# Three changes of order in a one-core encoder layer: a bank's read among the last quarter's scalings, three couples of differences at later blocks, and one more piece of filler in two turns of a scan

## The chip, the cores and the metric

The kernel runs on one core of a Trainium2 chip. The time is that of one execution on the device, in microseconds (us). Three runs of the kernel before gave 2434.46, 2435.89 and 2437.45; the median is 2435.89. The profile is of a further execution.

## The reference

One step of a one-layer hybrid encoder on 1024 new tokens of a prompt and 64 tokens of a running stream, which the kernel treats as T = 1088 columns; D = 1024. Cut to what matters:

```python
proj = rmsnorm(x) @ w_in                      # z | xBC | dt | q | k | v | g_ssm | g_att
xs, b, c = split(silu(causal_conv(xBC)))      # conv of width 4
for chunk in chunks_of_64(t):                 # state-space scan, 4 groups of 8 heads
    y     = (c b^T * decay) @ (dt x) + (c @ state) * exp(acum)
    state = state * exp(acum_end) + b^T @ (to_end * dt x)
y   = rmsnorm_per_group((y + d * xs) * silu(z))
o   = rmsnorm(differential_attention(q, k, v))
mix = sigmoid(g_ssm) * (y @ w_branch_ssm) + sigmoid(g_att) * (o @ w_branch_attn)
x   = x + mix @ w_out
ha, hb = split(rmsnorm(x) @ w_up)             # 2 x 2816 wide
x   = x + (silu(causal_conv(ha)) * hb) @ w_down
```

## The kernel before

Matrices lie with features on the 128 partitions and tokens along the free axis. Every large product is done in three passes of TensorE (PE): each operand is split into a high and a low part (a cast on ScalarE, ACT, L155 or L419, and a subtraction on VectorE, DVE, L156 or L420), and high x high, high x low and low x high are summed in one bank. A product in the text below is one matmul of 272 columns (a quarter of T). The in-projections of q, k and z, the up-projection and the down-projection also use a seven-product scheme for 2 x 2 blocks (`PARTS`), which needs differences of the four blocks as operands.

A scheduler sets the order of each engine's instructions from the program and from priorities; `issue_after` (the helper `after`) pins an instruction behind another. The queues of DMA issues are on SyncE (SP); each works in order.

**Scan** (about 1087 to 1498 us). Twelve spans: four groups `g`, each over three stretches of tokens of 384, 384 and 320 (`WIDE`). A span has three steps of a chunk of 128 tokens (the last one 64), and one more turn at its end, 48 turns in all. For a chunk, `front` transposes x (`tr`, L1280, and `xx`, L1289), forms the small product `cb` (L1282, L1283) and the decays `bc` (L1290 to L1293); `back` makes `yi` (L1301), `ye` (L1307) and the state's update `stp` (L1313, L1320), and puts y together (L1308, L1309). At a span's end `gated` adds d x (L1327), multiplies by silu(z) on GpSimd (POOL, L1328), squares (L1329) and sums (L1330, L1331); `normed` sums over partitions on PE (`gst`, L1335) and takes the root (L1338, L254 to L258); `scaled` scales (L1345) and stores y to `y_sc` (L1348 for groups 2 and 3; L1354 to L1357, with a split, for groups 0 and 1). Tile `y` has two buffers.

After each turn, `fill` takes work from a generator `filler` and issues it as PE work beside the scan: first the rest of the gates, then branch 1 (attention's output by its weights) and branch 2 (the first two groups of `y_sc` by theirs). A piece is 24 products (L170 to L172), and a turn takes 1.4 x 363 / 272 = 1.87 pieces on average. What is left runs after the scan, and then branch 3 (groups 2 and 3 of `y_sc`, loaded at L218 as b, split at L419 and L420), whose operations end in tanh gates on ACT (L226).

**Norm and up-projection** (about 1712 to 2190 us). `norm(q)` for each quarter of the tokens is a generator: the root, a pause, then eight scalings (L1527). `differences(s)` makes the block differences (L1537 to L1546) and their splits. `pair(f)` works through the 14 products groups (p, s) of one pair of blocks (L1612); its banks are copied or read by DVE, the read of p = 1 at L1639.

**Down-projection** (about 2182 to 2427 us). Three groups of 8, 8 and 6 feature blocks; four output blocks for each, twelve values of `i`, about 22 us each in the first two groups. Right operands for a group are loaded by `right_part` (L1721) from `h_sc` (plain) or `t_sc` (differences), in units called n, m and ph; ph shares its buffers (tag "fb") with the tile `ht`. `differences_of` makes the differences for a couple of blocks: load ht (L1689), two differences (L1693, L1694), two more (L1697, L1698), store to `t_sc` (L1700). The last three couples, which only the third group of the down-projection reads, are made during i = 0, 1 and 2. Banks are read at L1791, L1796, L1798, L1800, L1805 and L1808.

Of the kernel before, what the change touches and what calls it, by code (L numbers as in the profile page):

```python
# [12 lines left out]
ALU = mybir.AluOpType  # L13
# [6 lines left out]
KT = D // P  # L20
# [70 lines left out]
def hybrid_layer(ctx: ExitStack, tc: tile.TileContext, xT, xt, prm, cst, rope, wvd, win, wbs, wba, wout, wup, wdn,  # L91
# [31 lines left out]
    def col(o):  # L123
        return par[:, o : o + 1]
# [1123 lines left out]
    with (tc.tile_pool(name="sin", bufs=1) as sin, tc.tile_pool(name="sp", bufs=1) as sp,  # L1248
# [169 lines left out]
        def branch_tiles():  # L1418
            nonlocal bs
            cv_pool.release()  # L1420
            bs = tc.alloc_tile_pool(name="bs", bufs=1, side="right")
            yield from branch(True, side, o_sc, wba, D, (), store(m_sc))
            yield from branch(True, side, y_sc[: 2 * D], wbs[0], None, (), store(n_sc))

        bs, late = None, chain(filler, branch_tiles())
        for i in scan():
            if i == BRANCH_AT and late is not None:
                filler, late = late, None
            fill(SCAN_STEPS)
        load(out=conv, in_=conv_o)  # L1430
    dq.release()
    psf = ctx.enter_context(tc.tile_pool(name="psf", bufs=1, space=PSUM))
# [84 lines left out]
    def norm(q):  # L1517
        ps = psf.tile([P, 512], F32, name="st2", tag="st2")[:, :QW]
        for i, s in enumerate(sums[q]):
            PE.matmul(ps, ones, s, start=i == 0, stop=i == 1)  # L1520
        t = [row("fu", "n2") for _ in range(2)]
        rs = t[1][:, :QW]
        rstd_of(rows, rs, ps, QW, "n2", 1.0 / D, t=t)
        yield
        for k in range(KT):
            x = x1[q][k // 4][:, k % 4]
            V.scalar_tensor_tensor(x, x, col(O_FFN + k), rs, ALU.mult, ALU.mult)  # L1527

    def part(name, s, src):
        hi, lo = B[name, s] = [unit(*at) for at in home[name, s]]  # L1530
# [54 lines left out]
        left[0].update(coming)  # L1585
        run(firsts)
    next(fourth)
    run(fourth)
    run(differences(1))


    made.clear()
# [75 lines left out]

    early = [(p, s) for p in (0, 2) for s in range(2)]
    rest = [[(p, s) for p in (1, 3, 4, 5, 6)] for s in range(2)]  # L1670
    coming = up_parts(1)
    pairs = [begun(0), begun(1)]
    for at in early + rest[0]:
        pairs[0].send(at)
    for _ in range(2):
        more_left(1)
# [166 lines left out]
    for i in range(4 * len(DOWN)):  # L1843
# [8 lines left out]
        for at, (p, s) in enumerate(steps):  # L1852
            u.send((p, s))
            lefts_at(FT + i, at, blocks, token_major)
            if last:
                next(ahead_of)
            landed()
            if i in (0, 1, 2) and at in (1, 8, 10):
                if at == 1:
                    made_now = differences_of(*couples[len(couples) - 3 + i])  # L1860
                next(made_now, None)
        run(made_now)
        del left[FT + i]
# [106 lines left out]
```

## Time and profile before

| | us |
|---|---|
| runs | 2437.45, 2435.89, 2434.46 |
| profiled execution | 2433.65 |
| its span | 2431.9 |
| PE busy | 2390.7 |
| DVE busy | 1716.9 |
| ACT busy | 1213.1 |
| POOL busy | 692.3 |

Busy means that an instruction of the engine is running; a wait is time in which an engine's next instruction stands behind another engine or a transfer. "Granted clock" is the share of full TensorE speed in a stretch; over the whole span it was 0.996.

### The profile page before, as it was taken

The numbers are of one execution on the slowest core, as the hardware profiler recorded it, in microseconds if no ns is written. First come the engines' busy times: TensorE is split into PE (matmuls) and PEld (weight loads), VectorE is DVE, ScalarE is ACT, GpSimd is POOL, SyncE is SP. The second block draws the span as 40 slices with busy tenths as digits, with TensorE's granted clock in tenths as the row PEclk, the third lists the DMA queues.
The fourth block names the chain that finished last, engine by engine and source line by source line (L and its number), as shares of the span: only waits on it lengthen the run. The fifth ranks groups of instructions, "written<-read, shape, count | busy, mean of one in ns | idle before, by whom it ended". The sixth has DMA issues, their size and how long they took to land. (4 is left out here: it accounts for less than half of the span.)

```text
span 2431.9 us, 49445 instructions
## 1 busy us (share of the span) xinstructions
PE 2390.7 (98%) x18744; PEld 2317.6 (95%) x18744; DVE 1716.9 (71%) x3090; ACT 1213.1 (50%) x2683; POOL 692.3 (28%) x757
## 2 busy tenths in 40 slices
PE   8999999999999999999999999999999999999998
PEld 8999999999999999998899998999999999999998
DVE  4678887668687786867678665756866756777765
ACT  7344454356565665657655553434444333353442
POOL 0032433201011010115343332013254554443344
PEclk9999999999999999999999999999999999999999
DMA  7863768665444444336797954664124424357975
GB/s 244 278 236 129 268 204 302 197 194 155 155 150 152 127 149 142 108 127 227 261 329 248 334 177 162 213 210 159 56 85 147 156 97 157 126 185 211 254 182 105
DMA packets 296240, 449.79 MB, mean 185 GB/s; under 512 B 36729, under 2 KB 192514, under 8 KB 296002
## 3 DMA queue, kind: packets, MB, share of 16 engines
q1 hardware_dynamic: 284962, 420.31, 52.3%
q0 software_dynamic: 11040, 26.34, 5.3%
q8 instruction: 147, 2.41, 0.4%
q14 instruction: 91, 0.75, 0.1%
HBM read 294.03 MB, written 152.50 MB: 184 GB/s over the span
## 5 line engine op out<-in xcount | busy, mean ns | idle before, releaser
L170 PE MATMUL mm<-b,w_hi 128*128 128x272 f32 x1576 | 465.8, 296 | 0.0
L172 PE MATMUL mm<-b,w_lo 128*128 128x272 f32 x1576 | 459.3, 292 | 0.0
L171 PE MATMUL mm<-b,w_hi 128*128 128x272 f32 x1576 | 458.0, 291 | 0.0
L170 PEld LDWEIGHTS mm<-b,w_hi 128*128 128x128 f32 x1576 | 296.9, 188 | 6.2 <-issue 5.1
L171 PEld LDWEIGHTS mm<-b,w_hi 128*128 128x128 f32 x1576 | 297.1, 189 | 2.9 <-issue 2.1
L172 PEld LDWEIGHTS mm<-b,w_lo 128*128 128x128 f32 x1576 | 296.5, 188 | 0.7 <-issue 0.2
L996 DVE SCALAR_TENSOR_TENSOR cc<-pre,par,cc 128x272 f32<-128x272 f32 (+1 forms) x288 | 140.0, 490 | 16.0 <-ACT cc L994 13.0
L1612 PE MATMUL mx<-n,wh 128*128 128x272 f32 x1080 | 144.9, 290 | 1.9 <-DVE u L1639 1.2
L1612 PE MATMUL mx<-m,w_hi 128*128 128x272 f32 x752 | 144.6, 289 | 0.2 <-DVE m L420 0.2
L984 POOL COPY pre<-pre 128x3 f32<-128x3 f32 x72 | 22.9, 318 | 418.5 <-DVE cc L998 198.4
L1612 PEld LDWEIGHTS mx<-n,wh 128*128 128x128 f32 x1080 | 139.7, 190 | 2.3 <-DVE u L1639 1.4
L170 PE MATMUL mx<-b,w_hi 128*128 128x272 f32 x472 | 138.8, 294 | 1.1 <-ACT w_hi L155 0.5
L172 PE MATMUL mx<-b,w_lo 128*128 128x272 f32 x472 | 137.7, 293 | 1.0 <-DVE w_lo L156 1.0
L1120 ACT ACTIVATE p_t<-sc,mx 128x512 f32<-128x512 f32 (+6 forms) x144 | 106.2, 740 | 64.4 <-DVE mx L1111 30.7
L156 DVE TENSOR_TENSOR w_lo<-w_f,w_hi 128x1024 fp32r<-128x1024 f32 (+1 forms) x82 | 102.2, 1247 | 50.6 <-ACT w_hi L155 49.6
L420 DVE TENSOR_TENSOR wh<-w_f,wh 128x512 fp32r<-128x512 f32 (+1 forms) x144 | 136.7, 950 | 0.7 <-ACT wh L419 0.7
L171 PE MATMUL mx<-b,w_hi 128*128 128x272 f32 x472 | 135.8, 288 | 0.0
L155 ACT CAST w_hi<-w_f 128x1024 fp32r<-128x1024 f32 (+1 forms) x82 | 85.9, 1048 | 70.0 <-PE mm L171 49.3
L1612 PEld LDWEIGHTS mx<-m,w_hi 128*128 128x128 f32 x752 | 118.1, 188 | 0.4 <-DVE m L420 0.4
L563 POOL TENSOR_TENSOR ws<-w_f 128x512 f32<-128x512 f32 (+1 forms) x47 | 63.1, 1342 | 176.4 <-DMA w_f<-in_wdn_dram 61.7
L1621 ACT ACTIVATE cc<-pre,par 128x544 f32<-128x544 f32 (+1 forms) x44 | 37.2, 846 | 147.9 <-DVE pre L1656 147.2
L1612 PE MATMUL mx<-m,w_lo 128*128 128x272 f32 x376 | 108.3, 289 | 0.0
(460 smaller groups left out, 7074.3 us busy)
## 6 DMA issues: line engine op xcount, KB each, us to landing
w_f<-in_win_dram SPq DMA_DIRECT2D x48, 512.0 KB, 4.3
w_f<-in_wup_dram SPq DMA_DIRECT2D x80, 256.0 KB, 2.6
bc<-a_sc SPq DMA_DIRECT2D x32, 512.0 KB, 5.6
w_f<-in_win_dram SPq DMA_DIRECT2D x60, 256.0 KB, 3.8
b<-y_sc SPq DMA_DIRECT2D x24, 544.0 KB, 8.3
h_sc<-hb SPq DMA_DIRECT2D x44, 272.0 KB, 2.1
ht<-h_sc SPq DMA_DIRECT2D x22, 544.0 KB, 4.5
t_sc<-ht SPq DMA_DIRECT2D x22, 544.0 KB, 2.9
```

The costliest lines, as they stand in the source:

```text
L155: S.copy(hi, w)
L156: V.tensor_tensor(out=lo, in0=w, in1=hi, op=ALU.subtract)
L170: PE.matmul(ps, a_hi, b_hi, start=i == 0, stop=False)
L171: PE.matmul(ps, a_hi, b_lo, start=False, stop=False)
L172: PE.matmul(ps, a_lo, b_hi, start=False, stop=i == n - 1)
L420: V.tensor_tensor(out=lo, in0=src, in1=hi, op=ALU.subtract)
L563: G.tensor_tensor(out=s1, in0=q21, in1=q22, op=ALU.add)
L984: G.tensor_copy(pre[:, 0:3], tail)
L996: V.scalar_tensor_tensor(cc[:, :m], pre[:, i : i + m], cw(i), cc[:, :m], ALU.mult, ALU.add)
L1120: act(p_t[:n, :nk], sc[c][:n, :nk], AF.Exp, bias=mx[:n, c : c + 1], accum_out=dst)
L1612: PE.matmul(ps, w[x][:, c], b[y][:, k], start=start and k == i == 0, stop=k == 3 and i == 2, skip_group_check=not start)
L1621: act(cc[:, :n], pre[h][:, :n], AF.Identity, bias=col(O_FB + f), scale=cw(0))
```

## The change

Three edits. They leave every product and every operand as it was.

1. In the scan, turns 3 and 5 take one piece of filler more.
2. In the norm of the fourth quarter there is a pause ahead of the fifth scaling, and that scaling is pinned behind the last bank's read. The program runs this second half, and the differences that follow it, only after five product groups of the first pair have been issued.
3. The last three couples' differences are made during i = 1, 2 and 5 instead of 0, 1 and 2.

```diff
-        bs, late = None, chain(filler, branch_tiles())
+        bs, late, turn = None, chain(filler, branch_tiles()), 0
         for i in scan():
             if i == BRANCH_AT and late is not None:
                 filler, late = late, None
-            fill(SCAN_STEPS)
+            turn += 1
+            fill(SCAN_STEPS + (272 / UNIT if turn in (3, 5) else 0))
...
         for k in range(KT):
+            if q == 3 and k == KT // 2:
+                yield
             x = x1[q][k // 4][:, k % 4]
-            V.scalar_tensor_tensor(x, x, col(O_FFN + k), rs, ALU.mult, ALU.mult)
+            with after("read") if q == 3 and k == KT // 2 else ExitStack():
+                V.scalar_tensor_tensor(x, x, col(O_FFN + k), rs, ALU.mult, ALU.mult)
...
     next(fourth)
-    run(fourth)
-    run(differences(1))
+    next(fourth)
...
+    pairs = [begun(0), begun(1)]
+    for at in early + rest[0][:1]:
+        pairs[0].send(at)
+    run(fourth)
+    run(differences(1))
     coming = up_parts(1)
-    pairs = [begun(0), begun(1)]
-    for at in early + rest[0]:
+    for at in rest[0][1:]:
         pairs[0].send(at)
...
-            if i in (0, 1, 2) and at in (1, 8, 10):
+            if i in (1, 2, 5) and at in (1, 8, 10):
                 if at == 1:
-                    made_now = differences_of(*couples[len(couples) - 3 + i])
+                    made_now = differences_of(*couples[len(couples) - 3 + (1, 2, 5).index(i)])
```

In the built program the lines behind the first edit are one higher than before, those behind the second four, and those behind the new block of the program from three to seven.

PE at the end of the scan, before: the back half of the scan's last chunk, with products of branches 1 and 2 (b) on both sides of it. Ninety-six products follow it ahead of the last gst (L1335), and then 120 more ahead of branch 3.

```order
9264 L172 MATMUL mm<-b_17767,w_lo 128x272
9265 L170 MATMUL mm<-b_17767,w_hi 128x272
9266 L171 MATMUL mm<-b_17768,w_hi 128x272
9267 L172 MATMUL mm<-b_17767,w_lo 128x272
9268 L1301 MATMUL yi<-bc,xx 64x64 x8
9269 L1307 MATMUL ye<-in,start 128x64 x4
9270 L1313 MATMUL stp<-xx,b_cb 128x512
9271 L170 MATMUL mm<-b_17773,w_hi 128x272
9272 L171 MATMUL mm<-b_17774,w_hi 128x272
9273 L172 MATMUL mm<-b_17773,w_lo 128x272
```

The same engine at the same place in the changed kernel. Rows 9480 and following are already products of branch 3 (b_19320 and b_19330); the last product of branch 2 is row 9473.

```order
9472 L171 MATMUL mm<-b_17594,w_hi 128x272
9473 L172 MATMUL mm<-b_17593,w_lo 128x272
9474 L1280 MATMUL tr<-con,in 128x128 x4
9475 L1282 MATMUL cb<-con,in 128x128
9476 L1283 MATMUL cb<-in 128x128
9477 L1307 MATMUL ye<-in,state 128x128 x4
9478 L1313 MATMUL stp<-xx,b_cb 128x512
9479 L1301 MATMUL yi<-bc,xx 64x128 x8
9480 L170 MATMUL mm<-b_19320,w_hi 128x272
9481 L171 MATMUL mm<-b_19321,w_hi 128x272
```

A little later in the changed kernel the last two chunks' back halves and the gst of the last span but one (384 wide) stand together; the gst of the last span (320 wide) follows at row 9526.

```order
9506 L172 MATMUL mm<-b_19320,w_lo 128x272
9507 L1313 MATMUL stp<-xx,b_cb 128x512
9508 L1307 MATMUL ye<-in,state 128x128 x4
9509 L1335 MATMUL gst<-zin,con 128x384
9510 L1313 MATMUL stp<-xx,b_cb 128x512
9511 L1301 MATMUL yi<-bc,xx 64x128 x8
9512 L1307 MATMUL ye<-in,start 128x64 x4
9513 L1301 MATMUL yi<-bc,xx 64x64 x8
9514 L170 MATMUL mm<-b_19322,w_hi 128x272
```

So the products of branches 1 and 2 now all stand ahead of the last three chunks' back halves, where before 216 of them stood behind the last one.

DVE at the fourth quarter's norm, before: the eight scalings (L1527), a weight's split (L420) among them, then the read of the bank (L1639).

```order
1968 L1527 SCALAR_TENSOR_TENSOR x_21174<-x_21174,par,n_21811 128x272 x4
1969 L1527 SCALAR_TENSOR_TENSOR x_21639<-x_21639,par,n_21811 128x272
1970 L420 TENSOR_TENSOR w_lo<-ws_21681,w_hi 128x512
1971 L1527 SCALAR_TENSOR_TENSOR x_21639<-x_21639,par,n_21811 128x272 x3
1972 L1639 TENSOR_TENSOR u_21855<-mx,u_21854 128x272
1973 L1537 TENSOR_TENSOR x_20630<-x_21174,x_20630 128x1088
```

The same in the changed kernel, where the scaling's line is L1531, the read's L1642 and the first difference's L1541:

```order
1961 L1531 SCALAR_TENSOR_TENSOR x_21174<-x_21174,par,n_21811 128x272 x4
1962 L1531 SCALAR_TENSOR_TENSOR x_21639<-x_21639,par,n_21811 128x272
1963 L420 TENSOR_TENSOR w_lo<-ws_21681,w_hi 128x512
1964 L1531 SCALAR_TENSOR_TENSOR x_21639<-x_21639,par,n_21811 128x272 x2
1965 L1642 TENSOR_TENSOR u_21826<-mm,u_21825 128x272
1966 L1531 SCALAR_TENSOR_TENSOR x_21639<-x_21639,par,n_21811 128x272
1967 L1541 TENSOR_TENSOR x_20630<-x_21174,x_20630 128x1088
```

The read now stands ahead of the last scaling.

SP's queue ahead of the third group of the down-projection, before: no load of ht is left, and loads of parts from t_sc and h_sc alternate.

```order
1263 L1721 DMA m_29193<-h_sc 128x3x272
1264 L1721 DMA m_29196<-t_sc 128x3x272
1265 L552 DMA w_f<-in_wdn_dram 128x512 x11
1266 L552 DMA w_f<-in_wdn_dram 128x384 x2
1267 L1721 DMA m_29215<-t_sc 128x3x272
1268 L552 DMA w_f<-in_wdn_dram 128x384
1269 L1721 DMA ph<-h_sc 128x3x272
1270 L1721 DMA ph<-t_sc 128x3x272
```

In the changed kernel (ht at L1696, its store at L1707, parts at L1728):

```order
1248 L1728 DMA m_29193<-h_sc 128x3x272
1249 L552 DMA w_f<-in_wdn_dram 128x512 x11
1250 L552 DMA w_f<-in_wdn_dram 128x384 x3
1251 L1696 DMA ht<-h_sc 128x1088 x2
1252 L552 DMA w_f<-in_wdn_dram 128x384
1253 L1728 DMA ph<-h_sc 128x3x272
1254 L1728 DMA n_29292<-h_sc 128x3x272
1255 L1728 DMA n_29311<-h_sc 128x3x272
1256 L1707 DMA t_sc<-ht 128x1088 x2
1257 L1728 DMA m_29375<-h_sc 128x3x272
1258 L1728 DMA ph<-t_sc 128x3x272
1259 L1728 DMA n_29272<-t_sc 128x3x272
```

The third couple's loads and stores have moved to here, and every load from t_sc for this group stands behind them.

## The prediction

> **What bounds the kernel now.** I read the page's span and busy times first, then TensorE's waits, then stretches around each wait, then the timeline there. The page:
>
> ```profile
> span 2431.9 us, 49445 instructions
> PE 2390.7 (98%) x18744; PEld 2317.6 (95%) x18744; DVE 1716.9 (71%) x3090; ACT 1213.1 (50%) x2683; POOL 692.3 (28%) x757
> ```
>
> TensorE (PE) is busy 98% of 2431.9 us, so an order can win only from 41 us without PE work and from the clock, and can lose wherever it lets PE run into work that isn't ready. The change keeps every product. The waits of PE that lie at the three edited places (engine, line, what it waited for, total us, times, longest):
>
> ```profile
> PE yi L1301 <- DVE y L1309: 2.7, 1, 2.7
> PE tr L1280 <- DMA in<-x_sc: 2.2, 2, 1.3
> PE mx L1612 <- DVE u L1639: 1.2, 1, 1.2
> PE mx L1612 <- ACT wh L419: 0.6, 1, 0.6
> PE mm L1786 <- DVE u L1800: 0.9, 1, 0.9
> PE mx L1786 <- DVE u L1791: 0.4, 1, 0.4
> ```
>
> The first two are in the scan (edit 1), the next two in the up-projection (edit 2), the last two in the down-projection (edit 3): 8.0 us in all. Stretches (us; busy and instructions of PE, PEld, DVE, ACT, POOL; granted clock; DMA share; GB/s):
>
> ```profile
> 1500.00:1620.00 120.00, 118.46 (x933) 117.58 (x932) 77.36 (x152) 49.32 (x93) 0.00 (x0) 1.00 0.68 209
> 1160.87:1164.28 3.41, 0.71 (x7) 0.52 (x7) 1.38 (x2) 0.93 (x2) 0.00 (x0) 1.00 0.91 301
> 1164.28:1167.70 3.42, 3.42 (x24) 3.09 (x24) 0.00 (x0) 3.34 (x9) 2.19 (x2) 0.50 0.87 334
> 1727.48:1730.89 3.41, 3.21 (x14) 3.22 (x15) 3.41 (x6) 1.10 (x1) 0.00 (x0) 0.50 0.00 0
> 2201.94:2205.35 3.41, 1.70 (x9) 1.04 (x9) 3.41 (x5) 1.39 (x4) 1.45 (x2) 1.00 0.41 61
> 2205.35:2208.76 3.41, 3.41 (x18) 3.41 (x17) 3.38 (x7) 0.62 (x1) 0.00 (x0) 0.50 0.52 146
> ```
>
> The first row gives the price of one product of 272 columns in steady work: 118.46 / 933 = 0.127 us. The others show that a wait costs more than itself: the stretch ahead of 1164.28 had 0.71 us of PE work and the one ahead of 2205.35 had 1.70, and behind each, as behind the waits at 1727, a stretch of 3.41 us ran at clock 0.50. That costs 3.41 / 2 = 1.7 us a time.
>
> [...]
>
> **Edit 1, early scan: a gain.** Why yi waited:
>
> ```profile
> 1157.32 0.37 SPq L1357 DMA_DIRECT2D y_sc<-y  x1
> 1162.61 0.69 DVE L1308 TENSOR_TENSOR y<-ye,e 128x512 f32<-128x512 f32 x1 [1.86 <-DMA y_sc<-y]
> 1164.17 1.91 PE L1301 MATMUL yi<-bc,xx 128*64 128x128 f32 x16 [2.70 <-DVE y L1309]
> ```
>
> The store of span 0's y (1157.32, landed about 1162.6) frees the buffer that L1308 writes; the next yi sits behind L1309. In the new order PE has 64 products before the next yi instead of 27 (counted in the order), 37 x 0.127 = 4.7 us more cover there, and later gaps of 48 to 120 products. That covers 2.7 and the tr wait (1.3 of the 2.2) before it. Gain: 2.7 + 1.3 + 1.7 (clock) = 5.7 us; with the start gaps around the two waits about 6. Nothing in between gets late, since tr and cb now stand a whole chunk ahead of their yi. Ends: 4 (no clock) and 8. I take 6.
>
> **Edit 1, the scan's end: a loss, and the term that decides.** Two more pieces early shift all later scan turns back behind products. Before, the last yi stands 96 products ahead of the last gst, and 120 further products follow before any product reads the scan's last output. In the new order the products of gates and of branches 1 and 2 are used up while the tr and cb of a turn, three back halves (yi, ye, stp) and the gst of the last two spans are still to come. Between them stand only 36 products of branch 3; then 108 more; then the half of branch 3 that needs the last span. Prices, in the order of the chain (start, us):
>
> ```profile
> 1482.39 0.68 PE L1301 MATMUL yi<-bc,xx 64*64 64x64 f32 x16
> 1485.09 0.39 PE L170 MATMUL mm<-b,w_hi 128*128 128x272 f32 x1
> 1485.88 1.94 DVE L1327 SCALAR_TENSOR_TENSOR y<-in,par,y 128x320 f32<-128x320 f32 x4
> 1487.89 2.96 POOL L1328 TENSOR_TENSOR y<-y,zin 128x1280 f32<-128x1280 f32 x1 [11.79 <-DVE y L1327]
> 1490.88 1.27 ACT L1329 ACTIVATE zin<-y 128x1280 f32<-128x1280 f32 x1 [1.26 <-POOL y L1328]
> 1492.23 1.57 POOL L1330 TENSOR_TENSOR zin<-zin 128x640 f32<-128x640 f32 x1 [1.39 <-ACT zin L1329]
> 1493.88 0.87 POOL L1331 TENSOR_TENSOR zin<-zin 128x320 f32<-128x320 f32 x1
> 1498.04 0.43 ACT L1338 COPY grs<-gst 128x320 f32<-128x320 f32 x1 [5.61 <-PE gst L1335]
> 1501.23 1.94 DVE L1345 SCALAR_TENSOR_TENSOR y<-y,par,grs 128x320 f32<-128x320 f32 x4
> 1503.23 0.36 SPq L1348 DMA_DIRECT2D y_sc<-y  x1
> 1503.88 1.11 ACT L419 CAST b<-b 128x1088 fp32r<-128x1088 f32 x1 [1.65 <-DMA b<-y_sc]
> 1505.02 1.29 DVE L420 TENSOR_TENSOR b<-b,b 128x1088 fp32r<-128x1088 f32 x1 [1.85 <-ACT b L419]
> 1508.92 0.86 SPq L218 DMA_DIRECT2D b<-y_sc  x1
> 1523.99 1.28 ACT L226 ACT_TABLE_LOAD   x1
> ```
>
> And, of the loads L218 here, issue to landing:
>
> ```profile
> DMA to landing us min/median/max: 3.7/6.0/6.8
> ```
>
> The chain in the new order, t = 0 when PE has done its last product of branch 2:
> - the span of 384 before the last: yi to L1327 as here 1482.39 to 1487.82, 5.4; L1328 to L1331 from 1487.89 to 1494.75, 6.9. At 320 columns that is 12.3, at 384 up to 14.8; its turn is part done at t = 0, so its gst comes at about 12.
> - its norm and scaling, L1338's start to L1345's end, 5.1 here, x 1.2 = 6.2. ACT now has tanh between these functions, so two of its five new table loads (five in the order, 1.28 each) fall into it: 2.6. At 20.8 DVE is free for the last span.
> - its L1327, 1.9, and L1328 to L1331, 6.9: the last gst at about 30.
> - norm and scaling again, 5.1 + 2.6; the store of y to the next load's issue 5.7 (1503.23 to 1508.92); load 3.7 to 6.8; cast and L420 2.4. The last half of branch 3 can start at 50 to 53.
>
> PE's own work in that time: 144 products x 0.127 = 18.3, three back halves x 2.7 (1482.39 to 1485.09) = 8.1, tr, cb and two gst about 1: 27 us. PE thus loses 23 to 26 us, most of it in front of the last gst, where 36 products cover 4.6 us. From this goes the 1.5 us that PE is idle between 1500 and 1620 now. The first 12 us are the least certain, since parts of that span can be done before t = 0. Floor: one norm, then L1327 to gst (6.2 + 1.9 + 6.9 = 15) against 2 us of products, 13. I take 20, ends 13 and 25; if products still covered the chain, it would be 0.
>
> **Edit 2, the bank's read.**
>
> ```profile
> 1725.95 1.32 DVE L1527 SCALAR_TENSOR_TENSOR x<-x,par,n 128x272 f32<-128x272 f32 x3
> 1727.19 0.43 DVE L1639 TENSOR_TENSOR u<-mx,u 128x272 f32<-128x272 f32 x1
> ```
>
> In the built order the read moves ahead of one scaling only, the eighth: 1.32 / 3 = 0.44 earlier. The other L420 splits behind keep their order, DVE has no gap there (3.41 of 3.41 from 1727), and PE's next operand comes from it at the same time as before. So PE waits later what it waits less here: 0. Ends: a gain of 0.44 + 1.7 = 2.1 if the clock stays up and nothing absorbs it, and a loss of 0.4 for the scaling.
>
> **Edit 3, the three couples later.**
>
> ```profile
> 2201.60 1.44 DVE L1693 TENSOR_TENSOR ht<-ht 128x544 f32<-128x544 f32 x1
> 2339.24 0.38 SPq L1721 DMA_DIRECT2D m<-t_sc  x1
> 2361.53 1.29 PE L1786 MATMUL mm<-ph,wh 128*128 128x272 f32 x9
> ht<-h_sc SPq DMA_DIRECT2D x22, 544.0 KB, 4.5
> t_sc<-ht SPq DMA_DIRECT2D x22, 544.0 KB, 2.9
> ```
>
> Gain: of the first couple's four differences only one, L1693 at 2201.60, stands ahead of the waits for u (L1800). With it gone DVE is 1.44 us earlier there, and the wait of 0.9 goes. PE work in 2201.94 to 2205.35 rises from 1.70 to over 2.5 us, so the stretch at 0.50 behind it should go too: 0.9 + 1.7 = 2.6. Ends 0.9 (clock falls all the same) and 3.1. I take 2.5.
>
> Cost: the third couple's tile ht shares its buffers with the ph parts of the group at work, which come free only in that group's last block. In SP's new order its loads stand behind all 14 weight loads there, about where the t_sc loads begin now (2339.24), and every t_sc load of the next group stands behind its stores. Loads 4.5, four differences of at most 1.44 = 5.8, stores 2.9: t_sc can be read from about 2339 + 13 = 2352. A ph load, cast and split take about 7 more (3.7 to 6.8 and 2.4, the nearest rows): 2359, while PE first reads ph at 2361.53. Eight such parts follow one another, PE takes 1.29 us for each, and a queue that lets each pass in 1.5 to 2 us falls behind by 0 to 6. The last slack is 2.5 us, so 0 to 8; I take 3. What is queued behind the waiting stores on SP are these part loads, and PE waits for them.
>
> **Sum.** Against the profiled execution of 2433.65 us (span 2431.9 and 1.75 around it): -6 + 20 + 0 - 2.5 + 3 = +14.5, that is 2448. The median of the runs before is 2435.89, 2.2 above it; so I forecast 2450 us. By the ends taken alone, each at a time, 2441 to 2460.
>
> **Rivals.**
> - *The tail stays covered (not slower).* Place: the last two spans of the scan. The chain runs on DVE, ACT and POOL, which have fewer gate operations there than now; if it took no more than PE's own 27 us, the tail would cost nothing. For it: ACT and DVE are busy 50% and 71% only, and PE has to wait just where they are free. Against: the rows sum to 50 us, and even the floor exceeds the 4.6 us in front of the last gst. Price: -6 - 2.5 and 0 to 3 for edit 3: 2427 to 2430. It decides from a chain of 27 + 6 = 33 us downward. Chance 0.16.
> - *The couple's stores come later still (slower than forecast).* If the ht loads wait beyond 2339, each us goes through to PE once the slack of 2.5 is used: 10 us instead of 3 with the tail as forecast, 2457 to 2466. For it: SP serves its queue in order and ph needs the same buffers. Against: the order leaves them free by then. Chance 0.12.
> - *Losses and gains cancel.* PE has a tail of only some 6 us, because much of the last two spans is done earlier than I count: 2433 to 2438. Chance 0.08.
> [...]
>
> That the change doesn't do what it says holds for edit 2 only: the read passes one scaling, not four; its term is 0 already.
>
> **Numbers.** Forecast 0.64, 2441 to 2460. A measurement of this kernel tells about 0.2% (4.9 us) from no change. Faster by more: the first rival, 0.16, and a little of the third and of the forecast's low end, 0.18. Same: 0.08. Slower: 0.74. The range goes from 2429, in the middle of the first rival, to 2461.
>
> **What would show it.** Right: in the profile after, no wait of yi for y of more than 1 us before 1200, and clock 1.00 there; between about 1490 and 1550 waits of PE for xx, bc, zin or grs, or b from y_sc, of some 20 us together; ACT table loads between L254 and L255; at 2200 to 2208 clock 1.00; a wait of PE for ph, m or n near the third group of the down-projection. Wrong: a busy PE from 1490 to 1550, or the y wait at the early scan still there. The prediction fails as a whole if PE's waits between 1490 and 1550 are under 8 us.

## The result, and the profile after

The changed kernel takes 2470.15 us (median of 4 runs, 2469.25 to 2470.82) against 2435.5 before: a ratio of 1.015 (95% interval 1.0137 to 1.0164), 34.7 us more. (The ratios here and below are estimated from all runs of a session and differ a little from the quotient of the medians, 1.014 here.) The sign is as forecast; the size is more than twice the forecast 14.5, and 9 us above the range's end of 2461.

The page of the changed kernel, span and busy times:

```profile
span 2468.7 us, 49433 instructions
PE 2401.7 (97%) x18744; PEld 2324.3 (94%) x18744; DVE 1712.8 (69%) x3090; ACT 1219.0 (49%) x2687; POOL 694.9 (28%) x757
```

PE has the same 18744 matmuls. Its idle time grew from 41 to 67 us, and it is "busy" 11 us longer for the same work; the scan's end below, where PE was busy 41.3 us at a mean clock of 0.72 with work priced at 27 us, is more than enough for that. PE's waits, those that are new or changed at the three places (the lines of the scan are as before, those of the up-projection three and those of the down-projection seven higher):

```profile
PE mm L170 <- ACT b L419: 11.6, 2, 11.1
PE mx L1793 <- ACT m L419: 7.9, 1, 7.9
PE gst L1335 <- POOL zin L1331: 3.5, 2, 3.3
PE mm L172 <- DVE w_lo L156: 2.8, 1, 2.8
PE mx L1793 <- DVE n L420: 2.6, 1, 2.6
PE mm L1615 <- ACT m L419: 1.2, 1, 1.2
PE mx L1615 <- DVE u L1642: 0.6, 1, 0.6
```

The wait of yi for y (2.7) is gone, as forecast. Waits for b, gst and w_lo stand at the end of the scan, the waits for m and n in the down-projection.

Where the time lies can be read from the timelines: PE has the same matmuls in each stage, so the starts of the stages (first tr, first matmul of the up-projection, first of the down-projection, and there every 168 matmuls, or 126 in the last group, as a block, up to the start of the last) give the shares.

| us | before | changed | edit 1 alone | edit 2 alone | edit 3 alone |
|---|---|---|---|---|---|
| scan to output projection | 625.2 | 651.1 | 652.1 | 623.9 | 625.1 |
| up-projection | 469.4 | 470.9 | 469.8 | 469.7 | 469.4 |
| block 0 | 28.0 | 25.2 | 28.1 | 28.3 | 24.7 |
| blocks 1 to 3 | 63.3 | 63.3 | 63.4 | 63.6 | 63.6 |
| block 4 | 21.9 | 25.6 | 23.8 | 23.5 | 24.0 |
| blocks 5 to 7 | 63.3 | 63.3 | 63.3 | 63.3 | 63.3 |
| block 8 | 16.2 | 25.6 | 16.3 | 16.2 | 26.1 |
| blocks 9 to 11 | 47.2 | 47.2 | 47.2 | 47.2 | 47.2 |

The scan with what follows costs 26 us, block 8 another 9.4; block 0 gives 2.9 back. The scan's 26 us are a small gain and a large loss. The gain, by the stretch from the scan's start to just before its last turns (the single row before, the first of the next two after):

```profile
1085.00:1497.40 412.40, 407.23 (x3288) 371.11 (x3287) 281.78 (x351) 232.14 (x551) 155.06 (x104) 1.00 0.74 249
```

```profile
1085.00:1495.00 410.00, 408.10 (x3295) 374.73 (x3295) 248.59 (x323) 229.92 (x544) 139.43 (x96) 1.00 0.76 250
1495.80:1556.90 61.10, 41.33 (x243) 33.19 (x242) 35.57 (x56) 23.76 (x36) 16.91 (x9) 0.72 0.44 142
```

PE's idle time there fell from 5.2 to 1.9 us, 3.3 us won. The stretch at half clock at 1164 (1.7 by the prediction's price) is gone too, 5 us together, where 6 was forecast; but that stretch is also missing in the profiles of the second and of the third edit alone, where the scan's order is the old one and yi still waits 2.6 and 3.3 us, so its going is not shown to be this edit's. The last row is the scan's end, from the last product of branch 2 to the first product that needs the last span. PE was to do 27 us of work there; it took 61.1, at a mean clock of 0.72: a loss of 34. In detail, the timeline of that stretch (t = 0 at 1495.8):

```profile
1499.26 2.19 DVE L1327 SCALAR_TENSOR_TENSOR y<-in,par,y 128x384 f32<-128x384 f32 x4
1501.53 3.44 POOL L1328 TENSOR_TENSOR y<-y,zin 128x1536 f32<-128x1536 f32 x1 [5.40 <-DVE y L1327]
1502.51 3.54 DVE L156 TENSOR_TENSOR w_lo<-w_f,w_hi 128x1024 fp32r<-128x1024 f32 x1
1507.86 2.02 POOL L1318 TENSOR_TENSOR state<-state,decs 128x512 f32<-128x512 f32 x1 [2.89 <-DVE state L1320]
1509.85 2.26 POOL L1330 TENSOR_TENSOR zin<-zin 128x768 f32<-128x768 f32 x1
1512.19 2.62 POOL L1331 TENSOR_TENSOR zin<-zin 128x384 f32<-128x384 f32 x1
1514.87 1.01 PE L1335 MATMUL gst<-zin,con 128*128 128x384 f32 x1 [3.31 <-POOL zin L1331]
1523.76 2.20 DVE L1345 SCALAR_TENSOR_TENSOR y<-y,par,grs 128x384 f32<-128x384 f32 x4
1525.87 1.93 DVE L1327 SCALAR_TENSOR_TENSOR y<-in,par,y 128x320 f32<-128x320 f32 x4
1525.98 0.38 SPq L1348 DMA_DIRECT2D y_sc<-y  x1
1533.29 1.10 ACT L419 CAST b<-b 128x1088 fp32r<-128x1088 f32 x1 [1.22 <-DMA b<-y_sc]
1533.76 0.86 POOL L1331 TENSOR_TENSOR zin<-zin 128x320 f32<-128x320 f32 x1
1534.44 0.60 PE L170 MATMUL mm<-b,w_hi 128*128 128x272 f32 x1 [11.06 <-ACT b L419]
1538.48 1.27 PE L1335 MATMUL gst<-zin,con 128*128 128x320 f32 x2
1556.88 0.39 PE L170 MATMUL mm<-b,w_hi 128*128 128x272 f32 x1 [0.51 <-ACT b L419]
```

Against the chain of the prediction: the first gst came at 19.1, not 12, since on POOL a state update (L1318) stands ahead of L1330, and L1330 and L1331 took 2.26 and 2.62 us. L1318 waited for L1320 on DVE, which stood behind the split L156; that took 3.54 us beside L1328, where the one before it (1498.13) took 1.21. L1345 ended at 30.2, not 20.8: 1.7 us of that is the gst itself (L1338 on ACT starts at 1516.55), which the prediction's sum leaves out. From there the last L1331 ended at 38.8, 8.6 later, as added up (8.8). The last gst came at 42.7, not 30: 12 products of branch 3 stand ahead of it in PE's queue, and they wait for the y of the span before, stored only at 1525.98. From gst to the second half of branch 3 it took 18.4, not 20 to 23; norm and scaling took the forecast 7.7, but from the store's issue (1547.54) to the next load's (1551.11) it was 3.6 us, not 5.7.

The clock in that stretch, in windows of 3.41 us:

```profile
1504.37:1507.78 3.41, 1.53 (x10) 1.31 (x10) 3.41 (x4) 1.92 (x2) 0.60 (x1) 1.00 0.98 325
1507.78:1511.19 3.41, 3.35 (x9) 2.00 (x10) 3.41 (x5) 1.43 (x2) 3.33 (x2) 0.50 0.59 232
1511.19:1514.61 3.42, 0.36 (x3) 0.17 (x2) 3.37 (x5) 0.00 (x0) 3.34 (x2) 1.00 0.21 79
1514.61:1518.02 3.41, 3.15 (x4) 1.00 (x4) 0.00 (x0) 1.45 (x2) 1.20 (x2) 0.50 0.00 0
1518.02:1521.43 3.41, 3.41 (x22) 2.65 (x22) 1.43 (x3) 3.25 (x5) 0.00 (x0) 0.50 0.20 77
1524.84:1528.26 3.42, 0.00 (x0) 0.00 (x0) 2.97 (x7) 0.00 (x0) 0.37 (x1) 0.50 0.39 146
1541.91:1545.32 3.41, 3.41 (x17) 3.41 (x16) 0.88 (x2) 2.40 (x4) 0.00 (x0) 0.50 0.00 0
1545.32:1548.73 3.41, 3.41 (x29) 3.41 (x28) 3.23 (x8) 0.00 (x0) 0.00 (x0) 1.00 0.11 33
```

It is 0.50 in one window from 1507.78, behind one in which PE was busy for 1.53 us, and again from 1514.61 to 1545.32, nine windows in a row, behind one with 0.36 us. It returns behind a window in which PE was busy throughout (1541.91). But PE was busy throughout from 1518.02 as well, with small matmuls of the last turns, and the clock stayed at 0.50; what makes the difference is not shown.

The third edit's loss, on SP, ACT and PE in the changed kernel:

```profile
2367.72 0.86 SPq L1696 DMA_DIRECT2D ht<-h_sc  x2
2376.14 3.00 SPq L1707 DMA_DIRECT2D t_sc<-ht  x2
2381.55 2.14 SPq L1728 DMA_DIRECT2D m<-t_sc  x3
2393.99 0.87 ACT L419 CAST m<-m 128x816 fp32r<-128x816 f32 x1 [5.69 <-DMA m<-t_sc]
```

The third couple's ht is loaded 18 us before block 8 (which starts at 2385.8), its stores follow 8 us later, the loads from t_sc behind them, and PE waits 7.9 us for the cast of an m. That m is the second of the three in the row at 2381.55: it is issued at 2382.08 and lands at 2393.97. About 1.6 us of block 8's 9.4 are left beside the wait; the clock is 0.50 behind it, from 2391.8 to 2398.7.

### The profile page after: what moved, and what is told of

Same layout as the page of the kernel before. It is cut to its first block, busy times and chain, and to the rows that moved or that the text cites. A ratio compares the mean times of both kernels' runs of the same rounds, so it can differ in the third digit from the quotient of the medians.

```text
span 2468.7 us, 49433 instructions
## 1 busy us (share of the span) xinstructions
PE 2401.7 (97%) x18744; PEld 2324.3 (94%) x18744; DVE 1712.8 (69%) x3090; ACT 1219.0 (49%) x2687; POOL 694.9 (28%) x757
## 4 chain that ended last, share of the span: by engine, by line
PE 68%; DVE 5%; DMA 4%; issue 2%; POOL 1%; ACT 1%; SPq 0%; POOLq 0%; DVEq 0%; ACTq 0%
PE mx L1615 12%; PE mm L170 8%; PE mm L172 8%; PE mm L171 8%; PE mm L1615 5%; PE mx L1793 4%; PE po L1155 3%; PE mx L170 3%; PE mx L172 3%; PE mx L171 3%; PE sc L1106 2%; PE sc L1107 2%; PE mm L1793 2%; PE pt L1135 1%; PE yi L1301 1%
## 5 line engine op out<-in xcount | busy, mean ns | idle before, releaser
L170 PE MATMUL mm<-b,w_hi 128*128 128x272 f32 x1608 | 475.6, 296 | 11.6 <-ACT b L419 11.6
L172 PE MATMUL mm<-b,w_lo 128*128 128x272 f32 x1608 | 469.4, 292 | 2.8 <-DVE w_lo L156 2.8
L171 PE MATMUL mm<-b,w_hi 128*128 128x272 f32 x1608 | 467.8, 291 | 1.6 <-DVE b L420 1.6
L170 PEld LDWEIGHTS mm<-b,w_hi 128*128 128x128 f32 x1608 | 303.5, 189 | 15.6 <-ACT b L419 12.0
L171 PEld LDWEIGHTS mm<-b,w_hi 128*128 128x128 f32 x1608 | 303.7, 189 | 4.4 <-DVE b L420 2.1
L172 PEld LDWEIGHTS mm<-b,w_lo 128*128 128x128 f32 x1608 | 303.1, 189 | 4.1 <-DVE w_lo L156 3.1
L156 DVE TENSOR_TENSOR w_lo<-w_f,w_hi 128x1024 fp32r<-128x1024 f32 (+1 forms) x82 | 103.2, 1260 | 60.1 <-ACT w_hi L155 59.7
L1615 PE MATMUL mx<-m,w_hi 128*128 128x272 f32 x720 | 138.7, 289 | 0.2 <-DVE hb L1653 0.2
L420 DVE TENSOR_TENSOR wh<-w_f,wh 128x512 fp32r<-128x512 f32 (+1 forms) x144 | 136.7, 950 | 0.7 <-ACT wh L419 0.7
L170 PE MATMUL mx<-b,w_hi 128*128 128x272 f32 x440 | 130.6, 297 | 1.2 <-ACT w_hi L155 0.7
L172 PE MATMUL mx<-b,w_lo 128*128 128x272 f32 x440 | 129.4, 295 | 0.0
L171 PE MATMUL mx<-b,w_hi 128*128 128x272 f32 x440 | 127.7, 290 | 0.0
L1615 PEld LDWEIGHTS mx<-m,w_hi 128*128 128x128 f32 x720 | 113.1, 188 | 0.4 <-DVE hb L1653 0.4
L1632 POOL TENSOR_TENSOR hb<-hb,cc 128x544 f32<-128x544 f32 (+2 forms) x63 | 67.3, 1082 | 133.9 <-DVE hb L1653 98.1
```

What stands on the lines that cost most here:

```text
L156: V.tensor_tensor(out=lo, in0=w, in1=hi, op=ALU.subtract)
L170: PE.matmul(ps, a_hi, b_hi, start=i == 0, stop=False)
L171: PE.matmul(ps, a_hi, b_lo, start=False, stop=False)
L172: PE.matmul(ps, a_lo, b_hi, start=False, stop=i == n - 1)
L420: V.tensor_tensor(out=lo, in0=src, in1=hi, op=ALU.subtract)
L1615: PE.matmul(ps, w[x][:, c], b[y][:, k], start=start and k == i == 0, stop=k == 3 and i == 2, skip_group_check=not start)
```

## The experiments

**One edit at a time.** The first edit alone (scan_only):

> The first edit alone (one piece more in turns 3 and 5). From the two traces, measured at the start of the up-projection, the scan with what follows it takes 26.0 us longer in the changed kernel: the waits early in the scan are gone (about 7 us won) and the scan's last two spans lie bare (about 33 us lost). Theory A, all of this belongs to the first edit: 2435.5 + 26 = 2461.5. Rival B, a part of it comes from the other two edits, which change priorities and buffers further on in the program: under 2455.

Measured: 2458.49 us against 2432.93, ratio 1.0102 (1.0086 to 1.0118), 25.6 us more. The table above has its stages: the loss lies in the scan and what follows it. It is 3 us below Theory A's figure, and Rival B falls. The second edit alone (norm_only):

> The second edit alone (the last bank's read ahead of the fourth quarter's last scaling). My step: nothing, 2435.5 (bounds 2433.4 to 2436). The up-projection of the changed kernel took 1.5 us longer than before; if that belongs to this edit, 2437.

Measured: 2432.68 against 2432.93, ratio 1.0 (0.999 to 1.001): nothing that 2.4 us either way would show, as my step had it. The 1.5 us that the up-projection took longer in the changed kernel aren't this edit's: it is 0.3 us longer here, and among the kernels with the first edit and not the second it varies from 469.6 to 470.9. Its waits show how the earlier read is used up:

```profile
PE mx L1614 <- ACT m L419: 1.3, 1, 1.3
```

The wait for the bank's read falls from 1.2 to 0.5 us, and this wait for the cast of the next operand takes its place. The half clock behind that wait is no loss here either, though the prediction priced such a stretch at 1.7 us a time: with the old order the up-projection takes 469.4 us both in the profiles that have a stretch of 3.41 us at 0.50 there (before, nodep_before, couples_015) and in those that have none (couples_only, y3, couples_late0). The third edit alone (couples_only):

> The third edit alone (the last three couples during blocks 1, 2 and 5). In the changed kernel the first block of the down-projection is 2.9 us shorter, the fourth (counted from 0: i = 3 to 4) 3.7 longer and i = 8 9.4 longer. If these belong to the third edit alone: 2435.5 + 10.2 = 2445.7. If the late blocks were only late because the scan's loss had shifted them against something that runs on its own clock, 2433 to 2436.

Measured: 2444.2, ratio 1.004 (1.0024 to 1.0056), 11 us more by the medians. The gain in block 0 (3.3) and the loss in block 8 (9.9) are both there without the other edits. Block 0 has a second cause. In the twelve profiles with the first couple at its old place it took 26.1 to 26.5 us in the four without a stretch at half clock, 27.5 to 28.3 in the seven with one, and 29.1 in the one with two; with the couple later, 24.7 to 25.2, none with such a stretch. So the couple alone is worth about 1 to 1.8 us there, and the rest of the 3.3 is a half-clock stretch, which comes and goes without the edit as well. Block 4 can't be put down to this edit: it took 23.8 and 23.5 us with the first or the second alone, and 21.4 to 24.7 in all kernels with the first two couples at their old places and steps. So the extra 3.7 in the changed kernel isn't explained. The three parts add up to 25.6 + 0 + 11.3 = 37; all together cost 34.7 in a session where the kernel before had a median of 2435.5, and 36 to 37 against its medians in the later ones (2432.9 to 2434.3).

**How the scan's loss arises.** A smaller dose, one piece in turn 5 (scan_t5):

```diff
-            fill(SCAN_STEPS)
+            turn += 1
+            fill(SCAN_STEPS + (272 / UNIT if turn == 5 else 0))
```

> Only the scan, one piece more in turn 5 alone. The last yi then stands behind 6167 products and the last gst behind 6215, 25 ahead of branch 3, where before it was 6023 and 6119 and with two pieces more 6263 and 6275. Theory A (the loss grows with what is left of the scan when the products run out): of the chain of the last span, yi to gst of 12 us, 48 products cover 6; the way from the last gst to branch 3's second half, about 20 us, is covered by 133 products, 17 us; loss 6 + 3 = 9, and the early turns as with one piece more and one less (+2): 2444, between 2440 and 2448. Rival B (any shift of the whole scan costs the same, by another place in it): as with two pieces, 2458.

Measured: 2440.84 against 2433.12, ratio 1.0029 (1.0018 to 1.0039), 7.7 us more. PE's longest wait in the scan there:

```profile
PE gst L1335 <- POOL zin L1331: 8.5, 1, 8.5
```

The loss grows with how late the last turns stand, and it lies at the last gst, where Theory A puts it.

One piece more in turn 5, one less in turn 2 (scan_5m2: `272 / UNIT if turn == 5 else -272 / UNIT if turn == 2 else 0`):

> Only the scan: one piece more in turn 5 and one piece less in turn 2, the rest as before. In the built order the early turns then stand behind as many products as with one piece more (4247, 4343, 4391 products ahead of the sixth, seventh and eighth yi, where before it was 4232, 4319, 4367), but the last yi and the last gst stand where they stood before (6023 and 6119 of 7776). Theory A (the loss is the end of the scan, where no products are left to cover it; the gain is the early gap): faster than before by 3 to 7 us, 2429 to 2432. Rival B (shifting the scan's early turns costs by itself, by later loads or stores): 2436 or more.

Measured: 2435.52 against 2432.93, ratio 1.0009 (0.9997 to 1.0022). The last gst waits under 1 us, so the end of the scan cost nothing, but the gain did not come either: a miss for Theory A. Waits of the same sort stand elsewhere, the yi for L1309 still at 1165, the one for L1311 at 1303, in the middle of the scan:

```profile
PE tr L1280 <- DMA in<-x_sc: 3.3, 3, 1.4
PE yi L1301 <- ACT y L1311: 2.7, 1, 2.7
PE yi L1301 <- DVE y L1309: 1.4, 1, 1.4
```

So more products ahead of one yi do not by themselves win the 5 us. That the changed kernel wins them because all its turns stand further behind, which is what the end pays for, fits both and is not tested by itself.

The early wait by itself, with a third buffer for y (y3):

```diff
-                    y = sp.tile([P, 4, 384], F32, name="y", tag="y", bufs=2)
+                    y = sp.tile([P, 4, 384], F32, name="y", tag="y", bufs=3)
-BG = 8
+BG = 5
```

> The kernel before with a third buffer for the scan's y and, to make room, five instead of eight buffers for the gates' tiles (b_g); PE's order stays almost word for word. Theory A (yi at 1164 waits for the store of span 0's y only because there are two buffers, and the wait draws a stretch at half clock behind it): the wait of 2.7 us and the 1.7 behind it go, 4.4 us: 2428.5, unless the fewer b_g buffers cost something. Rival B (something else arrives as late, L1309 in front of it or the transfer of zin): within 1 us of before.

Measured: 2436.71 against 2433.78, ratio 1.0014 (1.0003 to 1.0026). The wait of yi is gone, and so is the stretch at half clock there, but these came:

```profile
PE cb L1282 <- ACT grs L1338: 3.4, 1, 3.4
PE mm L170 <- ACT w_hi L155: 2.4, 1, 2.4
```

The first stands at 1166.7, 82 us behind the scan's first tr, where the wait of yi stood 76 us behind it; the second is at 1588, after the scan, and whether it comes from the fewer buffers of the gates' tiles isn't shown. Theory A falls. Of Rival B the cause holds, that something else arrives as late close by, but not its size: the kernel is 2.9 us slower than before by the medians, outside both forecasts.

**Data or bare turns.** In the next two (nodep_before and nodep_scan), branch 3 reads other rows of y_sc than the layer needs, so their output is not the layer's:

```diff
-    run(branch(False, side, y_sc[2 * D :], wbs[1], 0, (n_sc, m_sc), mixed))
+    run(branch(False, side, y_sc[:D], wbs[1], 0, (n_sc, m_sc), mixed))
```

> The kernel before, but branch 3 reads the first 1024 rows of y_sc, which were stored long before, in place of the last 1024: its data don't depend on the end of the scan. It tells what the dependence costs before. Theory A: next to nothing, since 216 products stand behind the last yi: 0 to 2 us faster, 2431 to 2433. If it were more than 4 us faster, the end of the scan had been a bound already.

Measured: 2431.39 against 2433.12, ratio 0.9987 (0.9976 to 0.9998): the dependence cost next to nothing before.

> The first edit alone, and branch 3 reads the first 1024 rows of y_sc in place of the last 1024, as in the kernel above. The scan's last turns still stand bare in PE's order, without products between them, but no product waits for the last two spans. Theory A, in two shares: the 11 us that PE waits for a split of b behind the last yi and the waits for b and grs after it (3 us) go, the bare turns stay (about 15 to 20 us): 2458.5 - 14 = 2444, between 2440 and 2448. Rival B (the loss is the bare turns alone, the wait for b only took their place): 2455 or more. Rival C (the loss is the data of branch 3 alone): 2428 to 2432.

Measured: 2454.8, ratio 1.0078 (1.0063 to 1.0093). That is 3.7 us less than the first edit alone by the medians of two sessions, where I expected 14.

```profile
PE gst L1335 <- POOL zin L1331: 14.6, 3, 13.9
```

The 11 us wait for b is gone, and in the same place PE waits 13.9 us for the last gst's input. So the wait for b hid the longer chain behind it: what costs is that the last span's way from yi to gst lies bare. Rival B's 2455 holds to within the noise, Theory A's split into shares is wrong.

That way with other engines: the first edit, with gated's POOL work of the last two spans on DVE (scan_vec):

```diff
+            by = V if g == 3 and c else G
-            G.tensor_tensor(out=y, in0=y, in1=zt, op=ALU.mult)
+            by.tensor_tensor(out=y, in0=y, in1=zt, op=ALU.mult)
...
-            G.tensor_tensor(out=zt[:, 0:2], in0=zt[:, 0:2], in1=zt[:, 2:4], op=ALU.add)
-            G.tensor_tensor(out=zt[:, 0], in0=zt[:, 0], in1=zt[:, 1], op=ALU.add)
+            by.tensor_tensor(out=zt[:, 0:2], in0=zt[:, 0:2], in1=zt[:, 2:4], op=ALU.add)
+            by.tensor_tensor(out=zt[:, 0], in0=zt[:, 0], in1=zt[:, 1], op=ALU.add)
```

> The first edit alone, and for the last two spans the products and sums of gated (L1328, L1330, L1331) run on DVE instead of POOL. The scheduler then puts both gst directly behind the back halves, ahead of the 12 products of branch 3. Theory A (the loss is the chain from the last yi to the gst, which lies bare): on DVE these three take by their sizes about 1.5 + 0.8 + 0.45 us in place of 2.96 + 1.57 + 0.87, and the span before no longer queues behind the state's updates on POOL (about 5 us); 6 to 9 us less than the first edit alone: 2450. Rival B (PE itself, at half clock in that stretch, sets the time): under 2 us less, 2457.

Measured: 2453.97, ratio 1.0082 (1.0067 to 1.0097), 4.5 us less than the first edit alone, between the two forecasts.

```profile
PE gst L1336 <- DVE zin L1332: 9.9, 1, 9.9
```

PE now waits 9.9 us for the last gst's input, where the first edit alone had it wait 11.0 for b. Why, the rows of DVE and PE tell:

```profile
1523.52 1.94 DVE L1327 SCALAR_TENSOR_TENSOR y<-in,par,y 128x320 f32<-128x320 f32 x4
1529.29 2.21 DVE L1346 SCALAR_TENSOR_TENSOR y<-y,par,grs 128x384 f32<-128x384 f32 x4
1532.26 0.49 DVE L1332 TENSOR_TENSOR zin<-zin 128x320 f32<-128x320 f32 x1
1532.90 1.41 PE L1336 MATMUL gst<-zin,con 128*128 128x320 f32 x2 [9.89 <-DVE zin L1332]
```

The operations are shorter on DVE (0.49 for 0.86), but the way from L1327 to the last sum is not: 9.2 us, where the changed kernel has 8.7, because the scaling of the span before now stands among them. What went is queueing: L1327 of the last span no longer stands behind that scaling, and the last gst no longer behind 12 products of branch 3. So this run shows that the order of the queues sets a part of the loss; a shorter chain by itself it doesn't test.

**The clock's share.** The tail ran at half clock, which I had priced at nothing there. The first edit, with ten matmuls more whose result is thrown away, in the longest wait (scan_warm), and the first edit alone beside it (scan_only_b):

```diff
+            if g == 3 and c + w == T:
+                with after("yi"):
+                    for _ in range(10):
+                        PE.matmul(ps, ones, xs[:, 0, :w], start=True, stop=True)
             PE.matmul(ps, ones, zt[:, 0], start=True, stop=True)
```

> The first edit alone, with ten matmuls more whose result is thrown away, pinned behind the last yi, ahead of the 12 products of branch 3 and the last gst. They take about 8 to 10 us (0.4 us a pass at full clock, two passes each) and lie in the 11 us in which PE waits there. In the changed kernel the granted clock is 0.50 from 1514.6 to 1545.3, through this wait. Theory A (the half clock after the wait costs: 2.2 us in 108 products, 1.7 in the 12, 0.9 in the gst): with PE busy in the wait the clock comes back earlier and the kernel is 3 to 5 us faster than with the first edit alone, although it does more work: 2454. Rival B (the clock matters little, the chain sets the time): the same or slower, up to 3 us.

> The first edit alone once more, on the same chip as the kernel with ten matmuls more, as what that is compared with: 2458.5, between 2456 and 2460.

Measured on the same chip, against 2434.34: 2459.8 with the ten matmuls (ratio 1.0109, 1.0094 to 1.0125), 2461.1 without (1.0114, 1.0097 to 1.0131). The 108 products behind the last gst, first with, then without them (the second window begins at 1543.90):

```profile
1539.30:1553.00 13.70, 13.69 (x108) 13.67 (x108) 7.40 (x18) 5.12 (x8) 0.00 (x0) 1.00 0.36 108
```

```profile
1543.90:1560.40 16.50, 15.85 (x108) 15.63 (x108) 8.12 (x20) 6.28 (x10) 0.00 (x0) 0.86 0.48 148
```

With the ten matmuls they run at full clock and take 2.8 us less. But the next product, in the kernel with the ten matmuls, then waits for b:

```profile
1555.55 0.39 PE L170 MATMUL mm<-b,w_hi 128*128 128x272 f32 x1 [2.35 <-ACT b L419]
```

It waits 2.35 us there (0.62 without), so most of the time comes back, and the whole times can't be told apart: Rival B. For these 108 products the low clock is a companion of the loss; the chain through DVE, ACT, POOL and the transfers sets its size. But the ten matmuls brought the clock back only for a while. The 12 products ahead of the last gst ran at 0.50 here too:

```profile
1533.50:1537.50 4.00, 3.22 (x12) 2.92 (x13) 1.29 (x1) 0.00 (x0) 0.13 (x1) 0.50 0.00 0
```

These 12 and the gst lie on the chain, 1.7 and 0.9 us by the expectation's estimate, and the back halves ahead of the wait ran at 0.50 as well. What the clock costs there was not tried.

**Which couple costs.** The third alone at block 5, `i in (0, 1, 5)` (couples_015):

> Only the third couple moved, blocks 0, 1 and 5. Theory A: block 8 9.9 us longer, block 0 as before: 2443. Rival B (the loss comes from the first two couples being a block later): block 8 as before, 2433.

Measured: 2441.26 against 2433.78, ratio 1.0026 (1.0017 to 1.0036). Block 8 took 26.6 us, block 0 27.7.

```profile
PE mm L1786 <- ACT m L419: 7.7, 1, 7.7
```

The third couple's place makes the loss in block 8. A block later than before for each, `i in (1, 2, 3)` (couples_123):

> Only the couples, at blocks 1, 2 and 3 instead of 1, 2 and 5. Theory A (what costs at i = 8 is that the third couple's tile gets its buffer only when the second group's ph parts are done with, after block 6): block 8 as before, 16 us, and block 0 3.3 us shorter: 2430. Rival B (any couple later than block 2 collides with the loads of the next group): block 8 or block 4 some 4 to 10 us longer, 2437 to 2443.

Measured: 2446.55 against 2433.78, ratio 1.0053 (1.004 to 1.0067). Block 0 took 24.7 and block 8 16.2, but block 4 41.2:

```profile
PE mm L1786 <- ACT ph L419: 5.7, 1, 5.7
PE mx L1786 <- ACT w_hi L419: 3.5, 1, 3.5
```

Now the couple's tile takes the buffer from the second group's ph parts, as a cast of ph shows, which stands until the stores of ht have landed:

```profile
2284.93 1.10 ACT L419 CAST ph<-ph 128x1088 fp32r<-128x1088 f32 x1 [1.76 <-DMA t_sc<-ht]
```

Rival B's cause: at either place the couple collides with the loads of the group that comes next. Its size it misses: block 4 is 19 us longer, not 4 to 10, and the whole 3.6 above the forecast's end. Besides the waits, the clock is 0.50 for 20.5 us of that block.

And the couples in their old blocks, only the first one's steps later (4, 11 and 13 of block 0; couples_late0):

> Only the couples, in the blocks of the kernel before (i = 0, 1, 2), but the first couple's three parts in steps 4, 11 and 13 of block 0 instead of 1, 8 and 10. Theory A (the gain of the third edit is that the first couple's differences leave DVE's queue ahead of the waits in block 0; its loss is the later loads of the groups after): block 0 shorter by up to 2.9 us and no loss at i = 4 and i = 8: 2430. Rival B (the gain comes only with a whole block more between): 2433.

Measured: 2436.5 against 2433.12, ratio 1.001 (0.9997 to 1.0022). In its profile block 0 is 24.7 us and block 8 16.2, so block 0 gets as short without the late loads, as Theory A has it; in the whole time no gain can be told. Its scan, whose order is the same as before, took 3.5 us longer in that profile, and block 4 26.2: such differences between executions are as large as the gain.

No kernel tried here that computes the whole reference is faster than the kernel before by more than a measurement tells; the second edit alone, scan_5m2 and couples_late0 can't be told from it.

## Why the prediction was right in its sign and wrong in its size

- *Early scan, -6:* right in size, 3.3 us of idle time and perhaps the 1.7 of the clock. The 64 products instead of 27 that the prediction counts stand before the fifth yi; the one that waited, the eighth, has 4488 products ahead of it instead of 4368 by the traces, 120 more or 15 us, far more than the 4.7 of cover that it adds up. And scan_5m2 and y3 show that the place is not one wait with one cause: with that one taken away, another of the scan's waits comes in its place.
- *Scan's end, +20, ends 13 and 25:* this is the step that failed; it measured 34 less the 1.5 of before. The mechanism was right (scan_t5 and nodep_scan put it at the bare last turns), the term was mis-sized, and its upper end too. Three pieces of the chain were too short: the first gst at 12 instead of 19.1, because I put POOL's operations one behind the other without the state update between them and took the durations of L1330 and L1331 from the rows before (1.57 and 0.87 us in a span of 320, where here, in one of 384, they took 2.26 and 2.62); the norm behind it, 11.1 instead of 8.8, since the gst's own 1.7 us was left out; and the last gst waited for 12 products that stand in front of it, 3.9 us, which I had in the order and counted only as cover. The last part of the chain was a little shorter than I had it: the load at 1508.92, from which I took 5.7 us behind the store, cannot have waited for that store, which landed only 5.8 us after its issue at 1503.23. For the 108 products behind the last gst the unforeseen half clock is not one of the pieces: scan_warm took it away there, and the time stayed. In the 12 products ahead of the gst (3.9 us, which would be 1.5 at 0.127 each) and in the gst it is, by an unknown share. I also rounded the sum down, from 21 to 24 after the deduction to 20, on the thought that part of the first span would be done at t = 0; but its L1327 started only at 1499.26, 3.5 us behind t = 0, with the scaling of the span before (L1345) ahead of it on DVE.
- *Bank's read, 0:* right as far as can be told; 2432.68 against 2432.93.
- *First couple gone from block 0, -2.5:* right in the profile, 2.9 in the changed kernel and 3.3 alone, the sum of a wait and a half-clock stretch as forecast; but four profiles lack that stretch with the couple at its old place, so the second part was partly luck.
- *Third couple late, +3, ends 0 and 8:* mechanism right, size wrong; 9.4 and 9.9. The way from ht to the stores took 8.4 us, where I had 10.3. What I mis-sized was the load behind: eight loads from t_sc go out within 8 us (2380.47 to 2388.08), and the m that PE waits for, not the ph that I named, landed 11.9 us after its issue (2382.08 to 2393.97), where I had 3.7 to 6.8; the loads of the same stretch before took 4.3 to 6.9. From 2380 to 2399 the queues moved 297 GB/s, at which eight loads of 418 kB take 11 us (an estimate).
- Together 12.5 us of the 20 us missed are the scan's end, 6 to 7 the third couple. The rival with the couple's stores later still had the size for that term (10 us), though not its cause: the stores were about in time.
- The span of 2441 to 2460 that the prediction gives for the ends "each at a time" does not follow from them: one at a time they give 2443 to 2455. All upper ends together give 2464, still 6 us under the measured time.
- *The clock:* the prediction prices it by single stretches of 3.41 us at 0.50, and at the scan's end not at all, where there were nine in a row. In these windows it fell behind 1.53 us of PE work (1504.37) and 0.36 us (1511.19), and stayed at 1.00 behind 1.77 us (1500.95). It came back behind 3.35 us (1507.78) and 3.41 us (1541.91), and not behind the 3.41 us from 1518.02 to 1521.43. In the two windows without PE work (1524.84 and 1528.26) it was already low. What decides is not shown.
- *POOL's slow L1330 and L1331:* L1330 took 2.26 us at 768 columns with DVE at work beside it, where 1.57 us at 640 columns before would make 1.9 (an estimate by the columns); L1331 took 2.62 us at 384 columns, where 0.87 at 320 would make 1.04 (likewise). Over the twelve spans of the kernel before they took 1.54 to 2.63 us and 0.87 to 1.86 us. L156 on DVE took 3.54 us beside L1328 on POOL, and ended 1.1 us after it did (1504.97); in the kernel before, one beside L1328 (1489.38) took 2.55 us and one with POOL idle (1470.76) 1.23. What makes the longer rows longer is not shown.

## What to carry to other kernels

A wait at the front of a pipeline that is filled with spare work can be bought off with that spare work, but the bill comes at the end (here 3.3 us of idle time won and 34 us lost): count what is left to cover the last stage's whole chain, in the new order, before the gain is booked. Where a chain lies bare, every engine's queue counts with all that stands in it, and in-order work that looks like cover is a wait if its own data come from the same chain (11.1 us for b here). When several transfers are released at once, price the last of them by the queue and not by a lone transfer (the m of the eight loads landed after 11.9 us, where the loads of that stretch took 4.3 to 6.9 before). And compare a gain of one or two microseconds in one profile with other profiles of the same order: a half-clock stretch that comes and goes can be as large (about 1.5 us in block 0).

## What the runs showed that I had not expected

The clock stayed at 0.50 for 30.7 us in a row while PE did small pieces of work between waits, one window full of them included; bringing it back for the products behind the wait won nothing that can be told, because the next product then waited 2.35 us for its transfer and cast, against 0.62 without. A stretch at half clock need not cost anything: in block 0 it went with about 1.5 us, in the up-projection with none. And small edits moved the order far: one piece of 24 products in turn 5 moved the last yi from 6023 products to 6167, one each in turns 3 and 5 to 6263. Why it is so much more than the pieces themselves is not known.
